# A list schedule whose assumed interval of a TensorE product is replaced by the measured one

## The chip, the cores and the metric

The kernel runs on one core of one Trainium2 chip. The metric is the device time of one execution in microseconds; a set of runs is told by its median. Five engines matter: PE (TensorE, the products and the 128x128 transposes), ACT (ScalarE), DVE (VectorE), POOL (GpSimd) and SP, which here issues nearly all DMAs. Each works through its own queue in the order in which the program was written, and waits at an instruction whose inputs are not there.

## The reference

Two layers of a decoder trunk, 1024 positions, width 1024, float32:

```python
for layer in range(DEPTH):                              # DEPTH = 2
    h = rms_norm(x, ln_mix_pre[layer])
    m = even_mixer(...) if layer % 2 == 0 else odd_mixer(...)
    x = x + rms_norm(m, ln_mix_post[layer])
    h = rms_norm(x, ln_ffn_pre[layer])
    x = x + rms_norm(swiglu(h, ffn_w_gate[layer], ffn_w_up[layer], ffn_w_down[layer]), ln_ffn_post[layer])
```

The even mixer is causal pooling beside a gated unit, the odd mixer is sparse attention (eight heads) beside chunked retention (four heads). Both begin with an input projection and end with an output projection. The hidden width of swiglu is 2816.

## The kernel before

Every product is done three times on split operands (high times high, high times low, low times high), with 512 columns wherever possible. Positions are cut into eight row blocks of 128. A projection of a row block (`proj`, line 298 for the products) is four steps of six products. The swiglu products (lines 758 and 949) use a seven-product block scheme: `hidden` works on 22 slices of the hidden width, `seven` and `down` on the way back.

Between mixer and hidden stage stands what is called a tail here (`tail`, with `halves`): for each row block the second half of the output projection is evicted (line 1102, ACT), squared for its norm (350, ACT), multiplied by the gain (420, POOL), the inverse root is taken (357, POOL), the residual is added (423, DVE) and stored (426, SP), squared and rooted again, scaled in place (441, ACT) once the store has read it, then turned by transposes (540, PE) and split (546 ACT, 547 DVE). Row blocks 4 to 7 are also subtracted from blocks 0 to 3 (555, DVE and POOL). There are two such tails, one in each layer, and a simpler one between the layers (transposes of line 372).

The order of all of this isn't written by hand. Each step is a task with an engine, an assumed duration, a priority, dependencies and buffers (`Plan.add`). `Plan.run` plays a clock forward: whenever an engine is free it takes the ready task of best priority, lets it occupy the engine for its assumed duration, and makes its result visible a fixed latency later (0.2 us for PE). The order in which the tasks were taken is the order in which they are emitted, on all engines. A task of PE that has just become ready by another engine stands back for 0.4 us (`SLACK`). So an assumed duration decides which rows stand before which, and nothing else.

The assumed durations are functions of the number of columns: `t_pe` for products, `t_turn` 0.11 us for a transpose, and

```python
def t_act(n, ptr=0, sb=0): return 0.055 + n / 1200 + 0.093 * ptr + 0.04 * sb
def t_dve(n): return 0.068 + n / 960
def t_pool(n): return 0.15 + n / 475
```

`t_pe(512, 6)` is the duration of one step of `proj`, `t_pe(512, 12)` that of one product block of `hidden`, and `core` uses `t_pe` for its score and value products. The products of retention have durations written as numbers.

Of the kernel before, what the change touches and what calls it, by code (L numbers as in the profile page):

```python
# [157 lines left out]


def t_pe(n, k=1):  # L160
    return k * max(0.086 + n / 9000, n / 2400)


def t_turn(k):
# [19 lines left out]
class Trunk:  # L184
# [115 lines left out]
    def proj(s, x, i, ws, n, deps, last, ks=((0, 1), (2, 3), (4, 5), (6, 7)), whole=True):  # L300

        q, t = s.next(), None
        for j, kk in enumerate(ks):
            wt, wh, w = ws[kk[0] // 2]

            def fn(j=j, kk=kk, w=w):
                if j == 0:
                    x["pp"] = s.bank()
                for k in kk:
                    s.mm3(x["pp"][:, :n], [s.H[z][:, i, k, :] for z in range(2)], [z[:, sl(k % 2, n)] for z in w],  # L310
                          k == ks[0][0], k == ks[-1][-1])

            first = [w_[0] for w_ in ws] if j == 0 and whole else [wt]
            t = s.add("PE", t_pe(n, 6), fn, (8, q), [t, *first] + [d for k in kk for d in deps(k)], [wh] if last else [])
            if j == 0:
                x["hp"], ho = s.hold("b", t), s.hold("og", t)
        ho.n += 1
        t.rel.append(ho)
        return t

    def projT(s, x, h, w, out, deps, last, first=True, tag="b"):

        q, t = s.next(), None
        wt, wh, w = w
        for j in range(4):
            def fn(j=j):
                if j == 0 and first:
                    x["pp"] = s.bank(tag)
                for k in (2 * j, 2 * j + 1):
                    s.mm3(out(x["pp"]), [z[:, sl(k, P)] for z in w], [s.H[z][:, 4 * h:4 * h + 4, k, :] for z in range(2)],  # L330
                          k == 0, k == KD - 1)

            t = s.add("PE", t_pe(512, 6), fn, (8, q), [t, wt] + [d for k in (2 * j, 2 * j + 1) for d in deps(k)],
                      [wh] if last else [], after=x["first"] if j == 0 and not first else None)
            if j == 0 and first:
                x["first"], x["hp"] = t, s.hold(tag, t)
            if j == 0:
                ho = s.hold("og", t)
        ho.n += 1
        t.rel.append(ho)  # L340
        return t
# [391 lines left out]
    def hidden(s, l, B):  # L733
# [5 lines left out]
        for f in range(NF):  # L739
# [10 lines left out]
            def product(wn, c, vn, o, start, deps, rel=(), first=False, x=x, w=w, tag=tag):  # L750

                def fn():
                    if first:
                        x[o] = s.bank(tag[o])
                    out = x[o]
                    for k in range(4):
                        for j, (p, v) in enumerate(((0, 0), (0, 1), (1, 0))):
                            nc.tensor.matmul(out, w[wn][p][:, c + k * P:c + (k + 1) * P], V[vn](v, k),  # L758
                                             start=start and not (k or j), stop=k == 3 and j == 2,
                                             skip_group_check=not start)  # L760

                return s.add("PE", t_pe(512, 12), fn, (8, s.next()), [*deps, *tasks[vn]], rel)
# [1630 lines left out]
```

## Time and profile before

| | us |
|---|---|
| median of 3 runs | 2293.55 (2293.12 to 2297.48) |
| profiled execution, its own time | 2297.33 |
| span of the profiled execution, first to last instruction | 2295.6 |
| PE busy in it | 2236.2 |
| DVE, ACT, POOL busy | 1500.9, 1049.7, 938.7 |

The profiled execution is 3.78 us over the median, and 1.73 us of its time lie outside the span. The program has 11008 matmul records on PE. In time order the span holds: the even mixer (to about 230 us), the tail of layer 0 (to 288), its hidden stage (to 690), the way back (to 907), the tail between the layers (to 950), the input projections of the odd mixer (to 1079), retention (to 1237), retention and attention together and attention alone (to 1548), the output projection and the tail of layer 1 (to 1663), the hidden stage and the way back (to 2296).

A row of a timeline gives the start and the length of a run of like instructions, and in brackets how long the engine had been idle before it and who released it. A matmul's length includes its run-out, so that lengths overlap; intervals are read from start to start.

### The profile page before, as it was taken

The page shows a single profiled execution, that of the slowest core. Times are in us where ns is not written, and L with a number is a line of the kernel's source. Part 1 is how long each engine was busy: PE and PEld are TensorE (multiplying, and loading weights), DVE is VectorE, ACT ScalarE, POOL GpSimd, SP SyncE. Part 2 cuts the span into 40 slices and gives each one's busy share as a digit, 9 for nine tenths or more (in the row PEclk, how much of TensorE's full clock was granted, in tenths as well). Part 3 has the DMA queues.
Part 4 walks back from the last instruction along what each step waited for, and adds up shares of the span by engine and source line. Part 5 has one row for each costly group of instructions (what it writes and reads, how often), then busy time and mean ns, then how long its engine had stood idle before and what let it go on. Part 6 is the DMA issues. An engine that isn't in the chain of part 4 may idle for free.

```text
span 2295.6 us, 30648 instructions
## 1 busy us (share of the span) xinstructions
PE 2236.2 (97%) x11008; PEld 1871.6 (82%) x11008; DVE 1500.9 (65%) x2351; ACT 1049.7 (46%) x2107; POOL 938.7 (41%) x820
## 2 busy tenths in 40 slices
PE   9999899999999999999999999999899999999998
PEld 7888778888888787788888889988778888888887
DVE  6572765656546878554665789971676565646887
ACT  4252723333334434654445778872633333335442
POOL 4431655555532422301333545541665464612323
PEclk9999999999999999999999999999999999999999
DMA  4153532333334535421341000015533232334535
GB/s 165 60 203 101 202 129 101 107 104 103 106 112 142 182 124 179 142 92 49 122 149 45 13 22 11 29 36 179 171 129 115 92 115 92 115 114 139 178 118 180
DMA packets 109017, 262.07 MB, mean 114 GB/s; under 512 B 12593, under 2 KB 20929, under 8 KB 108866
## 3 DMA queue, kind: packets, MB, share of 16 engines
q1 hardware_dynamic: 108834, 260.11, 33.6%
q8 instruction: 87, 1.43, 0.3%
q14 instruction: 64, 0.52, 0.1%
q0 software_dynamic: 32, 0.01, 0.0%
HBM read 183.80 MB, written 76.28 MB: 113 GB/s over the span
## 4 chain that ended last, share of the span: by engine, by line
PE 80%; DVE 7%; ACT 6%; issue 3%; DMA 2%; POOL 2%; SPq 0%; DVEq 0%; POOLq 0%; ACTq 0%
PE b L298 21%; PE b L758 19%; PE e L758 15%; PE b L949 7%; PE e L949 7%; PE d L2098 2%; PE b L2212 2%; PE d L298 2%; PE b L2166 2%; DVE acc L423 1%; ACT W L2125 1%; DVE H L902 1%; ACT H L2182 1%; ACT junk L350 1%; PE b L1693 1%
## 5 line engine op out<-in xcount | busy, mean ns | idle before, releaser
L298 PE MATMUL b<-W,H 128*128 128x512 f32 (+1 forms) x2508 | 595.2, 390 | 5.0 <-DVE H L547 3.5
L298 PEld LDWEIGHTS b<-W,H 128*128 128x128 f32 x2508 | 450.8, 190 | 91.6 <-DVE H L547 4.3
L758 PE MATMUL b<-H,W 128*128 128x512 f32 x1440 | 341.7, 391 | 5.9 <-ACT acc L777 5.9
L758 PEld LDWEIGHTS b<-H,W 128*128 128x128 f32 x1440 | 271.2, 188 | 63.4 <-ACT acc L777 6.8
L949 PE MATMUL b<-H,H 128*128 128x512 f32 x608 | 187.3, 389 | 0.2 <-DVE H L902 0.2
L758 PE MATMUL e<-H,W 128*128 128x512 f32 x672 | 163.0, 391 | 2.0 <-DVE H L547 1.4
L626 POOL TENSOR_TENSOR raw<-x 128x512 f32<-128x512 f32 x40 | 84.1, 2102 | 195.6 <-DVE W L614 153.6
L611 ACT ACTIVATE W<-raw 128x1024 fp32r<-128x1024 f32 x80 | 85.0, 1062 | 161.8 <-PE b L758 77.9
L758 PE MATMUL e<-T,W 128*128 128x512 f32 x608 | 157.6, 389 | 0.0
L2135 POOL TENSOR_SCALAR W<-W,rc,gates 128x640 f32<-128x640 f32 (+7 forms) x128 | 101.8, 800 | 120.4 <-DVE rc L2131 90.7
L758 PEld LDWEIGHTS e<-H,W 128*128 128x128 f32 x672 | 125.5, 188 | 28.9 <-DVE H L547 2.1
L900 ACT ACTIVATE H<-x 128x1024 fp32r<-128x1024 f32 x88 | 73.2, 873 | 161.9 <-PE e L949 79.7
L949 PE MATMUL e<-H,H 128*128 128x512 f32 x456 | 142.1, 393 | 3.5 <-DVE H L902 3.5
L597 DVE TENSOR_TENSOR x<-x,g 128x1024 f32<-128x1024 f32 x80 | 140.6, 1759 | 6.8 <-DMA x<-in_w_gu 6.8
L825 POOL TENSOR_TENSOR acc<-acc,acc 128x512 f32<-128x512 f32 x57 | 123.6, 2169 | 37.4 <-DVE acc L803 36.2
L949 PEld LDWEIGHTS b<-H,H 128*128 128x128 f32 x608 | 114.0, 188 | 24.2 <-DVE H L902 0.6
L758 PEld LDWEIGHTS e<-T,W 128*128 128x128 f32 x608 | 114.1, 188 | 23.7
L758 PE MATMUL b<-T,W 128*128 128x512 f32 x536 | 130.7, 390 | 0.2
L902 DVE TENSOR_TENSOR H<-x,H 128x1024 fp32r<-128x1024 f32 x88 | 109.6, 1261 | 32.3 <-ACT H L900 32.3
L614 DVE TENSOR_TENSOR W<-raw,W 128x1024 fp32r<-128x1024 f32 x80 | 119.2, 1490 | 17.6 <-ACT W L611 17.3
L781 DVE TENSOR_TENSOR acc<-acc,b 128x512 f32<-128x512 f32 x44 | 30.2, 686 | 152.4 <-PE b L758 109.1
L883 POOL TENSOR_TENSOR W<-W,W 128x1024 f32<-128x1024 f32 (+1 forms) x24 | 56.7, 2390 | 169.6 <-DMA W<-in_w_down 144.7
(294 smaller groups left out, 4556.9 us busy)
## 6 DMA issues: line engine op xcount, KB each, us to landing
x<-in_w_gu SPq DMA_DIRECT2D x84, 512.0 KB, 3.7
hs<-acc SPq DMA_DIRECT2D x57, 512.0 KB, 2.8
x<-hs SPq DMA_DIRECT2D x49, 512.0 KB, 3.7
W<-pw SPq DMA_DIRECT2D x28, 512.0 KB, 4.1
xd<-acc SPq DMA_DIRECT2D x24, 512.0 KB, 3.7
x<-xd SPq DMA_DIRECT2D x24, 512.0 KB, 5.6
W<-in_w_down SPq DMA_DIRECT2D x19, 512.0 KB, 6.0
x<-hs SPq DMA_DIRECT2D x35, 256.0 KB, 3.6
```

Of the source, the lines that this page charges most:

```text
L298: s.nc.tensor.matmul(out, w[p], x[q], start=first and j == 0, stop=last and j == 2)
L597: nc.vector.tensor_tensor(v, v, s.g[:, l, :, None].to_broadcast([P, KD, P]), op=OP.mult)
L611: nc.scalar.activation(w[n][0], x[src][:, cols], AF.Copy)
L614: nc.vector.tensor_sub(w[n][1], x[src][:, cols], f32(w[n][0]))
L626: nc.gpsimd.tensor_tensor(x[n][:, sl(o, 512)], y[0], y[1], op=op)
L758: nc.tensor.matmul(out, w[wn][p][:, c + k * P:c + (k + 1) * P], V[vn](v, k), start=start and not (k or j), stop=k == 3 and j == 2, skip_gr ...
L825: nc.gpsimd.tensor_tensor(ss[o[0]][:, sl(o[1], 512)], *y, op=op)
L883: e.tensor_tensor(X[n, c][:, w], X[x1, c][:, w], X[x2, c][:, w], op=OP.subtract)
L900: order = t = s.add("ACT", t_act(512 * m, sb=1), lambda: nc.scalar.activation(z[0], src()[:, :512 * m], AF.Copy), (9, q), [*deps, *fr], af ...
L902: return s.add("DVE", t_dve(512 * m), lambda: nc.vector.tensor_sub(z[1], src()[:, :512 * m], f32(z[0])), (9, q), [t], rel), q_, z
L949: nc.tensor.matmul(banks[o, p], y[u][:, 512 * k + p * P:512 * k + (p + 1) * P], w[v][:, sl(k, 512)], start=fresh and n == 1, stop=n == 3 * ...
L2135: nc.gpsimd.tensor_scalar(dst, dst, d["rc"][:, x, j:j + 1], gate, op0=OP.mult, op1=OP.mult)
```

## The change

One line. The assumed interval of a product was the larger of 0.086 + n/9000 and n/2400 us, that is 0.2133 us for 512 columns, 0.1144 for 256 and 0.1002 for 128. It becomes the larger of 0.109 and 0.0134 + n/2400, that is 0.2267, 0.1201 and 0.109.

```diff
 def t_pe(n, k=1):
-    return k * max(0.086 + n / 9000, n / 2400)
+    return k * max(0.109, 0.0134 + n / 2400)
```

No instruction is added, taken away or changed. The order changes on all five engines. On PE it is the same in the hidden stages and on the way back; it differs in the even mixer, in the three tails, in retention and attention, and at the end of attention. Three places follow, first as before, then as changed. In names, the digits behind the last underscore are a buffer's number, given in the order of emission, so the same buffer can have another number.

PE, tail of layer 0. L298 rows are steps of the output projection (b_1962 before and b_2037 in the change are row block 7, the last; b_1917 is block 6), L540 rows are transposes of finished row blocks (acc_1588 is block 4, acc_1567 is block 3), L758 rows are the first block of the hidden stage. Before:

```order
L298 MATMUL b_1917<-W_1648,H_65 128x512
L540 MATMUL b_2022<-ident,acc_1588 128x128 x4
L298 MATMUL b_1962<-W_1419,H_64 128x512
...
L298 MATMUL b_1962<-W_1636,H_64 128x512
...
L540 MATMUL b_2055<-ident,acc_1445 128x128 x4
L298 MATMUL b_1962<-W_1648,H_64 128x512
...
L540 MATMUL b_2078<-ident,acc_1567 128x128 x4
L540 MATMUL b_2089<-ident,acc_1567 128x128 x4
L758 MATMUL e_2103<-H_64,W_1664 128x512
```

In the change:

```order
L540 MATMUL b_2013<-ident,acc_1588 128x128 x4
L540 MATMUL b_2022<-ident,acc_1567 128x128 x4
L540 MATMUL b_2030<-ident,acc_1567 128x128 x4
L298 MATMUL b_2037<-W_1398,H_64 128x512
...
L540 MATMUL b_2050<-ident,acc_1445 128x128 x4
L298 MATMUL b_2037<-W_1419,H_64 128x512
...
L758 MATMUL e_2070<-H_64,W_1664 128x512
...
L540 MATMUL b_2098<-ident,acc_1621 128x128 x4
L298 MATMUL b_2037<-W_1636,H_64 128x512
...
L540 MATMUL b_2117<-ident,acc_1497 128x128 x4
L298 MATMUL b_2037<-W_1648,H_64 128x512
```

The two transposes of block 3 stood behind the last step of the projection; now they stand ahead of all four steps of row block 7. The first hidden block (12 products) and a transpose set of block 5 (acc_1621) stand ahead of its third step, a set of block 1 (acc_1497) ahead of its last. The tail of layer 1 changes in the same way.

POOL, the same tail. L420 is the gain of a row block (acc_1675 is block 7, the last), L357 an inverse root, L555 a subtraction for blocks 5 and 6. Before:

```order
L420 TENSOR_TENSOR acc_1646<-acc_1646,x_275_1728 128x1024
L357 TENSOR_TENSOR rs_2075<-ms_2041,mhalf 128x1
L357 TENSOR_TENSOR rs_2087<-ms_2060,mhalf 128x1
L420 TENSOR_TENSOR acc_1675<-acc_1675,x_275_1728 128x1024
L555 TENSOR_TENSOR acc_1621<-acc_1621 128x512
```

In the change:

```order
L420 TENSOR_TENSOR acc_1646<-acc_1646,x_275_1728 128x1024
L357 TENSOR_TENSOR rs_2068<-ms_2055,mhalf 128x1
L357 TENSOR_TENSOR rs_2087<-ms_2035,mhalf 128x1
L555 TENSOR_TENSOR acc_1621<-acc_1621 128x512
L357 TENSOR_TENSOR rs_2115<-ms_2094,mhalf 128x1
L555 TENSOR_TENSOR acc_1497<-acc_1497,acc_1621 128x512
L555 TENSOR_TENSOR acc_1646<-acc_1646 128x512
L420 TENSOR_TENSOR acc_1675<-acc_1675,x_275_1728 128x1024
```

The gain of the last row block now stands behind three subtractions of earlier blocks that it stood ahead of.

PE, end of attention. L2166 and L2168 are the last transposes of probabilities, L2212 the value products (vs of the selected branch, x of the window branch, the last of all), L298 the output projection. Before:

```order
L2166 MATMUL b_14550<-ident,W_14460 128x128
L2168 MATMUL b_14550<-ident,cp_14416 128x128
L2212 MATMUL b_14553<-H_64,vs_7152 128x256
...
L298 MATMUL b_14539<-W_13924,H_64 128x512
...
L2212 MATMUL b_14553<-H_64,x_1062_7663 128x256
```

In the change:

```order
L298 MATMUL b_14496<-W_14002,H_64 128x512
...
L2166 MATMUL b_14579<-ident,W_14483 128x128
L2168 MATMUL b_14579<-ident,cp_14451 128x128
L2212 MATMUL b_14525<-H_64,x_1062_7663 128x256
L2212 MATMUL b_14525<-H_65,x_1062_7663 128x256
```

Ten value products and a step of the projection stood between the last transposes and the last value products; now nothing does.

## Rows read from the trace of the kernel before

**Rows 1.** The page, parts 1 and 2: engines' busy time; PE in 40 slices.

```profile
PE 2236.2 (97%) x11008; PEld 1871.6 (82%) x11008; DVE 1500.9 (65%) x2351; ACT 1049.7 (46%) x2107; POOL 938.7 (41%) x820
...
PE   9999899999999999999999999999899999999998
```

**Rows 2.** Busy time in stretches; columns as the first row names them.

```profile
core 0: us, PE busy (x) PEld busy (x) DVE busy (x) ACT busy (x) POOL busy (x), PEclk, DMA share, GB/s
233.90:288.00 54.10, 47.97 (x257) 38.53 (x256) 40.63 (x60) 40.40 (x72) 34.25 (x26) 1.00 0.56 195
...
907.20:949.70 42.50, 36.75 (x186) 28.64 (x185) 36.90 (x63) 33.41 (x56) 26.72 (x21) 1.00 0.62 215
...
1603.90:1662.70 58.80, 51.41 (x265) 40.73 (x264) 39.66 (x60) 41.81 (x73) 34.76 (x27) 0.97 0.55 186
1617.60:1620.90 3.30, 3.30 (x10) 2.56 (x9) 0.39 (x3) 2.21 (x5) 1.57 (x2) 0.50 0.92 325
...
1090.40:1237.00 146.60, 146.50 (x754) 121.49 (x753) 91.36 (x276) 59.76 (x162) 48.99 (x74) 1.00 0.34 115
1237.00:1541.50 304.50, 289.15 (x2086) 264.59 (x2084) 260.62 (x674) 250.29 (x772) 150.22 (x246) 0.99 0.07 22
```

**Rows 3.** Waits of PE over the span: us in total, times, longest.

```profile
PE b L758 <- ACT acc L777: 5.9, 2, 3.0
PE b L540 <- DVE H L547: 3.9, 4, 1.5
```

**Rows 4.** The chain that ended last, in time: start, length, what.

```profile
333.92 5.44 PE b L758 x24
```

**Rows 5.** The page, part 5: groups with busy us, mean ns of one.

```profile
L626 POOL TENSOR_TENSOR raw<-x 128x512 f32<-128x512 f32 x40 | 84.1, 2102 | 195.6 <-DVE W L614 153.6
...
L781 DVE TENSOR_TENSOR acc<-acc,b 128x512 f32<-128x512 f32 x44 | 30.2, 686 | 152.4 <-PE b L758 109.1
```

**Rows 6.** Timeline of PE in the tail of layer 0.

```profile
256.63 0.66 PE L540 MATMUL b<-ident,acc 128*128 128x128 f32 x4 [1.50 <-DVE H L547]
...
260.23 1.64 PE L298 MATMUL b<-W,H 128*128 128x512 f32 x6
261.71 1.03 PE L540 MATMUL b<-ident,acc 128*128 128x128 f32 x8
...
288.03 3.34 PE L758 MATMUL e<-T,W 128*128 128x512 f32 x14
```

**Rows 7.** Timeline of ACT in the tail of layer 0.

```profile
258.86 1.14 ACT L441 ACTIVATE acc<-acc,rs 128x1024 f32<-128x1024 f32 x1
...
261.91 0.60 ACT L1102 ACTIVATE acc<-b 128x512 f32<-128x512 f32 x1 [0.32 <-PE b L298]
...
263.36 1.07 ACT L350 ACTIVATE junk<-acc 128x1024 uint8<-128x1024 f32 x1
...
278.36 1.18 ACT L441 ACTIVATE acc<-acc,rs 128x1024 f32<-128x1024 f32 x1
```

**Rows 8.** Timeline of POOL in the tail of layer 0.

```profile
264.59 2.42 POOL L420 TENSOR_TENSOR acc<-acc,x 128x1024 f32<-128x1024 f32 x1 [1.78 <-ACT junk L350]
...
273.08 1.31 POOL L555 TENSOR_TENSOR acc<-acc 128x512 f32<-128x512 f32 x1 [1.77 <-DVE acc L555]
274.40 0.55 POOL L357 TENSOR_TENSOR rs<-ms,mhalf 128x1 f32<-128x1 f32 x1
```

**Rows 9.** Timeline of DVE in the tail of layer 0.

```profile
270.09 2.31 DVE L423 SCALAR_TENSOR_TENSOR acc<-acc,rs,x 128x1024 f32<-128x1024 f32 x1 [0.44 <-POOL rs L357]
```

**Rows 10.** The page, part 6: DMA issues, KB each, us to landing.

```profile
xd<-acc SPq DMA_DIRECT2D x24, 512.0 KB, 3.7
```

**Rows 11.** Timeline of PE at the end of attention.

```profile
1541.43 0.27 PE L2168 MATMUL b<-ident,cp 128*128 128x128 f32 x1
...
1544.13 1.36 PE L2212 MATMUL b<-H,x 128*128 128x256 f32 x10
```

**Rows 12.** Timeline of DVE at the end of attention.

```profile
1542.57 0.93 DVE L2186 TENSOR_TENSOR H<-b,H 128x128 fp32r<-128x128 f32 x3 [1.05 <-ACT H L2182]
```

## The prediction

> **What bounds the kernel now.** I read the busy times and slices first [rows 1]: PE is busy 2236.2 of 2295.6 us, and every slice shows an 8 or a 9. A busy PE also counts the run-out of matmuls, so I then looked at what one product takes where nothing is waited for: 24 products in 5.44 us [rows 4], 226.7 ns each. That is the new table's figure for 512 columns (226.7) and not the old one's (213.3). So the change makes the plan's PE truer, and since only the order of emission depends on it, the time changes only where PE waits today or will wait tomorrow.
>
> The windows show where it waits [rows 2]: 54.10 - 47.97 = 6.1 us idle in the tail of layer 0, 42.50 - 36.75 = 5.8 between the layers, 58.80 - 51.41 = 7.4 in the tail of layer 1, 304.50 - 289.15 = 15.4 in attention, and 146.60 - 146.50 = 0.1 in retention. The two waits of PE over the span that belong to a tail are short [rows 3]: 3.0 us at most for the first block after it, 1.5 at most for a transpose. In the hidden stages and on the way back PE's order stays as it was, and in the even mixer PE is full (the first slices are 9s, the fifth holds the tail); those I cost at nothing.
>
> The other engines are off the path in sum (DVE 1500.9, ACT 1049.7, POOL 938.7 us, [rows 1]), but their assumed durations are too short: the plan gives a DVE pass of 512 columns 0.068 + 512/960 = 0.601 us and the trace 0.686; it gives POOL 0.15 + 512/475 = 1.228 us for 512 columns and the trace shows 2.102 for the one at line 626 [rows 5]. Before, PE's figure was too short as well (213.3 for 226.7, 6%), and part of the error cancelled. Now only the others are too fast. The plan believes that evicted, normed and split data arrive earlier, counted in products, than they do, and puts their consumers on PE earlier. That is the reason why I look for losses and not for gains.
>
> **The tail of layer 0.** Before, the last step of the output projection starts at 260.23 and takes 1.64, so it ends at 261.87; then come the two transposes of block 3 [rows 6], whose input is scaled from 258.86 to 260.00 [rows 7]. In the change these stand ahead of all four steps of row block 7. PE stops there until 260.00 and everything behind comes after it. From there to the end of the projection stand 36 products (24 of the projection, 12 of the first hidden block) and about five sets of four transposes. Eight transposes take 1.03 us and four 0.66 [rows 6], so a set in a row of others adds 0.37. 36 x 0.2267 = 8.16, plus 5 x 0.37 = 1.9, on 260.00 makes 270.1. The last step ends 8.2 us later than before.
>
> PE does useful work in most of that delay (it runs the hidden block it would have run later), so what counts is when the last row block comes back. Its chain before: eviction 261.91, 0.60; square 263.36, 1.07 [rows 7]; gain 264.59, 2.42 [rows 8]; residual 270.09 to 272.40 [rows 9]; store, 3.7 to landing [rows 10]; scale 278.36 to 279.54 [rows 7]; 17.7 us from the last product to the scaled block. This chain had waits in it: between the gain's end at 267.01 and the addition at 270.09 lie 3.1 us, and between the addition's end and the scaling 6.0, where the store takes 3.7 and the second square and root run beside it. Without queues it is 0.60 + 1.07 + 2.42 + a root of 0.55 [rows 8] + 2.31 + 3.7 + 1.18 = 11.8, and with about 0.2 at each of seven handoffs (0.16 from the square's end at 264.43 to the gain) 13.2. From 270.1 that is 283.3, some 4 us later than 279.54. The gain now stands behind three subtractions on POOL; the one before it in the profile ran 273.08 to 274.39 [rows 8], so by the time of the last gain (about 272) they may hold it for 1 to 2 us; I count this within the 0.2 us steps.
>
> What needs this block is the rest of the hidden stage's first products: before, the 14 products of 288.03 start 8.5 us after the scaling, with transposes, splits and cover between. The change takes 12 products of cover (2.7 us) to the front, so I let the whole 4 through: **+4**. Bounds: if the transposes' input comes in time and POOL is free, 0; if the 17.7 us stay as they are, 270.1 + 17.7 = 287.8, +8.3.
>
> **The tail of layer 1.** The order moves in the same way; its idle time (7.4 us) is alike: **+4**, with the same bounds.
>
> **Half clock.** At 1617.60 to 1620.90 ten products fill 3.30 us at a granted clock of 0.50, that is 1.2 GHz [rows 2]; at 226.7 ns they would be 14.6, so such a stretch costs about 1.0 us. PE's waits grow in both tails, so one more of them is likely: **+1**, from 0 (none) to +4 (two in each tail).
>
> On the interval itself the Trainium skill has a figure. Its page "TensorE: Matmul & The Clock Gate", section "Wait — 56ns, not 53.3ns?", gives 215.7 ns from start to start for 512 columns at the full clock, which is nearer to the old table than to the new one. The trace has 226.7 over 24 products [rows 4], and the measurement decides. By the page the 36 products above would end 36 x 11 = 0.4 us earlier; the sum would be 0.8 less.
>
> **Between the layers.** The first block's transposes now stand ahead of three product steps, where the plan expects their input sooner. PE waits there, and the steps it would have run fill waits that follow today. 5.8 us are idle now; I take **+0.5**, from -2 (a third of that idle time filled) to +2.
>
> **Retention.** PE has no idle time there (0.1 of 146.6), so it can't gain. Transposes and score products come earlier in the row by about one step of six products (1.36 us), where the data of DVE (91.36 us of 146.6 busy) is seldom that early. Most of it stays covered: **+1**, from 0 to +4 (three times the loss of a step).
>
> **Attention.** 15.4 us are idle, spread over some 300; 289.15 of PE against 260.62 of DVE and 250.29 of ACT, in a long loop. Here products are of 256 columns and the table changes 5% (0.1144 to 0.1201), transposes keep 0.11. The order shuffles in both directions. **0**, from -6 to +6 (40% of the idle time either way).
>
> **End of attention.** The last transposes start at 1541.43 [rows 11]; the last split by DVE ends at 1542.57 + 0.93 = 1543.50 [rows 12]. Before, ten value products and a projection step lay between and covered these 2.1 us; now the ten last value products (1.36 us for ten, [rows 11]) follow at once. About eight of them don't need the last split, about 1.0 us: 2.1 - 1.0 = **+1**, from 0 to +2.
>
> **SP.** A few reads of weights move behind stores in SP's row. Weights have buffers ahead of their use, and I cost it at 0; without that cover a read issued late by one store's 3.7 us [rows 10] would cost PE that, once or twice. This stays in the range's upper end.
>
> **Sum.** 4 + 4 + 1 + 0.5 + 1 + 0 + 1 = +11.5. On the profile's own time 2297.33 that is 2308.8; that execution is 3.78 over the median 2293.55, so the forecast for a median is 2305. The likeliest case alone runs from about 2299 to 2309.
>
> **Rivals.**
> 1. *The tails' chain keeps its length.* The last row block's 17.7 us aren't queues but latency, POOL's subtractions take the place of the waits that vanish: +8.3 in each tail, 16.6, with 1 to 4 of half clock and the other terms' 2.5 this is +20 to +23, about 2315. For it: POOL is at 34.25 of 54.10 us in the tail [rows 2], and subtractions stand ahead of the gain. Against it: 3.1 us before the addition are plainly a queue that a later block doesn't meet.
> 2. *Nothing comes of it.* When PE waits, the engines behind it work off their queues, and the next wait is shorter by as much; in the tails the hidden block that is brought forward is work that PE would have done later anyhow. Then only the end of attention and half a step here and there remain, 0 to +4, about 2295. For it: PE is 97% busy and its work is the same; the tails lose 6 to 7 us now and hold a fixed amount of cover. Against it: the cover is moved in front of the step that starts the last chain.
> 3. *Faster.* The true interval makes the long loop of attention fit: the plan's PE there is 5% slower, so fewer steps of DVE and ACT are placed as if they were late, and half of the 15.4 us idle is filled, -7.7; the tails' delay stays covered by the hidden products. With +1 at the end of attention, 2293.55 - 6.7 = 2287. It decides if PE's idle time in attention falls under about 8 us. For it: 15.4 us is the largest idle time of any stage. Against it: DVE and ACT are assumed too fast there, and a slower PE makes that worse.
>
> **How the numbers follow.** Forecast 0.48, rival 1 0.14, rival 2 0.23, rival 3 0.15. 0.2% is 4.6 us, about what a measurement of this kernel can tell from no change: faster is under 2289, slower over 2298.1. The forecast and rival 1 lie on the slower side, with a little of rival 2 (0.02): 0.64. Of rival 2 remains 0.21 and of rival 3 0.01 within 0.2%: 0.22. Faster 0.14. The range takes in most of rival 1 (to 2316) and rival 2 down to 2290, and leaves out rival 3.
>
> **What would show it.** Right: in both tails the last projection step ends 8 to 9 us later, PE waits in front of block 3's transposes and again before the first products that need row block 7, and the hidden stage of layer 0 starts its even run about 4 us later; PE's idle time rises in the tails, not in the hidden stages; at the end of attention a wait of about 1 us for a split by DVE. Wrong: the last step ends later but the hidden stage starts as before (rival 2); the wait for row block 7 grows by 8 (rival 1); attention's span falls by more than 6 us (rival 3). If the time moves in a hidden stage or on a way back, where PE's order is unchanged, my reading is wrong altogether.

## The result, and the profile after

| | before | with the change |
|---|---|---|
| median, us | 2294.57 (4 runs, 2293.12 to 2297.48) | 2309.91 (4 runs, 2307.09 to 2312.32) |
| profiled execution, own time (span) | 2297.33 (2295.6) | 2307.09 (2305.4) |

The ratio is 1.0066, with a 95% interval of 1.0051 to 1.0081: 15 us slower. The two profiled executions lie only 9.8 us apart, since that of before is its slowest of four and that of the change its fastest. Single executions of one order differ by 4 to 9 us (23 runs of before beside the last experiments lie between 2290.61 and 2299.78); stages are therefore priced by medians, and the traces are read for places.

Of the page, PE's busy time (before in [rows 1]), and of part 5 two groups that answer to [rows 5]:

```profile
PE 2232.3 (97%) x11008; PEld 1869.5 (81%) x11008; DVE 1489.0 (65%) x2351; ACT 1051.7 (46%) x2107; POOL 916.4 (40%) x820
...
L626 POOL TENSOR_TENSOR raw<-x 128x512 f32<-128x512 f32 x40 | 71.1, 1778 | 222.6 <-DVE W L614 183.7
...
L781 DVE TENSOR_TENSOR acc<-acc,b 128x512 f32<-128x512 f32 x44 | 30.2, 687 | 151.1 <-PE b L758 107.8
```

PE does the same work in 9.8 us more. Its waits over the span (us in total, times, longest), against [rows 3]:

```profile
PE b L758 <- ACT acc L777: 7.4, 2, 3.7
PE b L2166 <- DVE H L2186: 6.8, 9, 2.3
PE b L298 <- DVE H L1377: 6.7, 1, 6.7
...
PE b L540 <- DVE H L547: 4.4, 2, 2.4
```

The third is new as a large one, and it stands in the even mixer. The same wait in a timeline of PE, before and after (start, length, what, in brackets the idle time before it and who ended it):

```profile
140.18 4.29 PE L298 MATMUL b<-H,W 128*128 128x512 f32 x18
145.16 0.97 PE L298 MATMUL b<-v,W 128*128 128x512 f32 x3 [0.69 <-DVE H L1377]
```

```profile
140.51 4.29 PE L298 MATMUL b<-H,W 128*128 128x512 f32 x18
151.46 2.90 PE L298 MATMUL b<-v,W 128*128 128x512 f32 x6 [6.66 <-DVE H L1377]
```

0.69 us of waiting have become 6.66, and the six products behind the wait take 2.70 us to the next start instead of 1.36. The stages by windows (columns as in [rows 2]; the same stretches, moved by what the trace is late there):

```profile
138.00:152.00 14.00, 7.34 (x31) 5.73 (x30) 14.00 (x14) 9.00 (x16) 9.35 (x6) 0.90 0.46 187
240.80:294.90 54.10, 47.18 (x256) 37.93 (x254) 35.75 (x58) 40.90 (x71) 33.19 (x26) 1.00 0.54 195
914.60:957.10 42.50, 36.80 (x186) 28.80 (x186) 36.57 (x66) 34.37 (x57) 26.84 (x21) 1.00 0.62 217
1612.40:1671.20 58.80, 52.27 (x279) 42.17 (x278) 36.50 (x60) 43.57 (x76) 33.15 (x26) 1.00 0.52 185
```

In the tails PE is idle about as long as before (6.9 us for 6.1, 6.5 for 7.4), between the layers too (5.7 for 5.8). The first row is the new hole, with the granted clock at 0.90 in its mean. The stretch at 0.50 that [rows 2] shows in the tail of layer 1 is not there (1.00 in the last row).

To follow the loss along the span I compared, in the two traces, when PE starts the work that stands behind the same sum of product intervals (0.2267 us for 512 columns, 0.120 for 256, 0.109 for 128). Late by, in us, positive where the change is later:

| up to | late by |
|---|---|
| the even mixer before the wait | -1.0 |
| its output projection | +6.9 |
| first hidden products (about 290 us) | +7.2 |
| even run of the hidden stage (from 350) | +9.4 |
| end of the way back | +7.4 |
| projections of the odd mixer | +5.7 |
| attention, first part (1320) | +2.8 |
| attention, 80 us before its end | +4.5 |
| output projection of layer 1 | +8.5 |
| hidden stage of layer 1 | +8.8 |
| end | +9.8 |

So in this pair the even mixer costs 8 us, the tail of layer 0 with the first hidden slices 2.5, the end of attention 4, the tail of layer 1 next to nothing, and the odd mixer gives 4 to 5 back before its end. The 2.0 us by which the change catches up on the way back of layer 0 are mostly clock: before has PE at a granted clock of 0.50 from 771.00 to 774.40, and the trace of the change has no such stretch there.

### The profile page after: what moved, and what is told of

Its sections match the earlier page's. It is cut to its first block, busy times and chain, and to the rows that moved or that the text cites. A ratio compares the mean times of both kernels' runs of the same rounds, so it can differ in the third digit from the quotient of the medians.

```text
span 2305.4 us, 30667 instructions
## 1 busy us (share of the span) xinstructions
PE 2232.3 (97%) x11008; PEld 1869.5 (81%) x11008; DVE 1489.0 (65%) x2351; ACT 1051.7 (46%) x2107; POOL 916.4 (40%) x820
## 5 line engine op out<-in xcount | busy, mean ns | idle before, releaser
L298 PE MATMUL b<-W,H 128*128 128x512 f32 (+1 forms) x2508 | 594.9, 389 | 1.9 <-ACT H L377 1.2
L298 PEld LDWEIGHTS b<-W,H 128*128 128x128 f32 x2508 | 449.3, 189 | 86.6 <-ACT H L377 1.6
L758 PE MATMUL b<-H,W 128*128 128x512 f32 x1440 | 343.2, 392 | 7.4 <-ACT acc L777 7.4
L758 PEld LDWEIGHTS b<-H,W 128*128 128x128 f32 x1440 | 272.4, 189 | 65.1 <-ACT acc L777 8.3
L758 PE MATMUL e<-H,W 128*128 128x512 f32 x672 | 162.5, 391 | 2.4 <-DVE acc L781 2.4
L626 POOL TENSOR_TENSOR raw<-x 128x512 f32<-128x512 f32 x40 | 71.1, 1778 | 222.6 <-DVE W L614 183.7
L758 PE MATMUL e<-T,W 128*128 128x512 f32 x608 | 157.9, 389 | 0.0
L597 DVE TENSOR_TENSOR x<-x,g 128x1024 f32<-128x1024 f32 x80 | 143.2, 1794 | 13.5 <-DMA x<-in_w_gu 13.3
L758 PEld LDWEIGHTS e<-H,W 128*128 128x128 f32 x672 | 125.5, 188 | 29.2 <-DVE acc L781 3.2
L758 PEld LDWEIGHTS e<-T,W 128*128 128x128 f32 x608 | 114.0, 188 | 23.6
L758 PE MATMUL b<-T,W 128*128 128x512 f32 x536 | 130.2, 389 | 0.0
L614 DVE TENSOR_TENSOR W<-raw,W 128x1024 fp32r<-128x1024 f32 x80 | 117.6, 1470 | 14.8 <-ACT W L611 14.8
L902 DVE TENSOR_TENSOR H<-x,H 128x1024 fp32r<-128x1024 f32 x88 | 102.9, 1184 | 34.8 <-ACT H L900 34.8
```

Source lines behind the costliest of these rows:

```text
L298: s.nc.tensor.matmul(out, w[p], x[q], start=first and j == 0, stop=last and j == 2)
L597: nc.vector.tensor_tensor(v, v, s.g[:, l, :, None].to_broadcast([P, KD, P]), op=OP.mult)
L614: nc.vector.tensor_sub(w[n][1], x[src][:, cols], f32(w[n][0]))
L626: nc.gpsimd.tensor_tensor(x[n][:, sl(o, 512)], y[0], y[1], op=op)
L902: return s.add("DVE", t_dve(512 * m), lambda: nc.vector.tensor_sub(z[1], src()[:, :512 * m], f32(z[0])), (9, q), [t], rel), q_, z
```

## The experiments

**One stage at a time.** Both intervals are kept for each product task, and the plan uses the new one only for a range of PE's 1581 tasks; outside it the order of every engine is that of before, inside that of the change.

```diff
 def t_pe(n, k=1):
-    return k * max(0.109, 0.0134 + n / 2400)
+    return Both(k * max(0.086 + n / 9000, n / 2400), k * max(0.109, 0.0134 + n / 2400))
...
-                    push(best, "end", now + best.dur)
+                    n += eng == "PE"
+                    dur = float(best.dur) if n < 155 else float(getattr(best.dur, "old", best.dur))
+                    push(best, "end", now + dur)
```

The condition is `n < 155` in only_even, `155 <= n < 420` in only_tail0, `420 <= n < 1255` in only_odd and `n >= 1255` in only_tail1.

only_even: 

> The new interval is used for the first 155 tasks of PE (through the even mixer, into its output projection), the old one behind; the order is that of the change up to there and that of before behind. Theory of the trace (a wait of 6.7 us before a product of the pooled branch): +6 to +8 us. Theory of the prediction (PE is full there, nothing happens): 0, within 2.

only_tail0: 

> The new interval is used for PE's tasks 155 to 419 only (tail and hidden stage of layer 0). Theory of the prediction: +4 to +5 us. Theory of the trace (the last projection step comes some 5 us later, but hidden products cover it, and about 2.5 us come from waits and half clock in the first hidden slices): +1 to +3.5.

only_odd: 

> The new interval is used for PE's tasks 420 to 1254 only (tail between the layers, projections of the odd mixer, retention, attention). Theory of the prediction: +2.5 us (0.5 + 1 + 0 + 1). Theory of the trace: losses at the end of attention of about 4 and gains before it of about 5, so -3 to +1.

only_tail1: 

> The new interval is used for PE's tasks from 1255 on (tail of layer 1 and what follows). Theory of the prediction: +4 to +5 us. Theory of the trace: +0 to +3. If the four runs add up to the whole difference (+15 us of the medians) the stages act each for itself; if they stay at about +10 (the difference of the two profiled executions), the rest lies in the spread of executions.

Measured against 2295.27 us of before (27 runs beside them):

| | median, us | difference | ratio, 95% interval |
|---|---|---|---|
| only_even | 2301.76 | +6.5 | 1.0027, 1.0015 to 1.0038 |
| only_tail0 | 2298.36 | +3.1 | 1.0017, 1.0008 to 1.0026 |
| only_odd | 2296.11 | +0.8 | 1.0005, 0.9996 to 1.0014 |
| only_tail1 | 2298.24 | +3.0 | 1.0015, 1.0006 to 1.0024 |

The differences add up to 13.4, the ratios to 1.0064; the whole change has 1.0066. Each difference is known to about 2 us; as far as that tells, the stages act each for itself. All four lie where the reading of the trace had put them, and the even mixer, priced at nothing in the prediction, is the largest.

**What the wait in the even mixer is made of.** VectorE from the last common point to the result that PE waits for (line 1377), in the change, and POOL beside it:

```profile
139.72 4.08 DVE L692 TENSOR_TENSOR acc<-x,acc 128x512 fp32r<-128x512 f32 x3
143.72 1.77 DVE L1340 TENSOR_TENSOR m<-m,gl 128x512 f32<-128x512 f32 x1
145.42 3.43 DVE L1360 TENSOR_TENSOR H<-m,H 128x512 fp32r<-128x512 f32 x2
148.77 0.68 DVE L1367 TENSOR_TENSOR v<-acc,v 128x512 fp32r<-128x512 f32 x1
...
150.58 0.74 DVE L1377 SCALAR_TENSOR_TENSOR H<-b,psc,H 128x512 fp32r<-128x512 f32 x1
```

```profile
141.58 1.68 POOL L704 TENSOR_TENSOR x<-x 128x512 f32<-128x512 f32 x1 [0.64 <-DVE acc L692]
143.33 3.29 POOL L704 TENSOR_TENSOR x<-x,x 128x512 f32<-128x512 f32 x2
146.70 1.60 POOL L704 TENSOR_TENSOR x<-x 128x512 f32<-128x512 f32 x1
```

Lines 685, 692 and 704 prepare the first two hidden slices ahead of time, work of the lowest priority. In the change the first of the three splits (the second slice's) stands ahead of VectorE's chain, and once it is done POOL's four sums start, at 141.58. Until they end at 148.30 the passes of 512 columns on VectorE take 1.7 us from start to start; from 148.77 on they take 0.60. POOL's passes start 1.7 us apart as well (141.58, 143.33, 146.70 with one between), where one alone is 1.3 us long, as if the two engines took turns. Before, that split ran at 151.81 and the sums behind it:

```profile
141.35 0.68 DVE L1360 TENSOR_TENSOR H<-m,H 128x512 fp32r<-128x512 f32 x1
141.95 0.68 DVE L1367 TENSOR_TENSOR v<-acc,v 128x512 fp32r<-128x512 f32 x1
...
144.36 0.74 DVE L1377 SCALAR_TENSOR_TENSOR H<-b,psc,H 128x512 fp32r<-128x512 f32 x1
```

To part the queue from the overlap, even_sums_late keeps the order of only_even on VectorE up to the wait, and puts a small copy on POOL in front of the sums that reads VectorE's late result:

```diff
+                if (h, g) == (0, 2):
+                    def gate():
+                        nc.gpsimd.tensor_copy(s.pad, f32(Hk(1, 2, 0))[:, 0, :8])
+                    t = s.add("POOL", 0.2, gate, (0, q), [Y[h, g]])
+                    t.users.append(s.first_sum)
+                    s.first_sum.wait += 1
```

> Like only_even (new interval for the first 155 PE tasks, order of the change there), but POOL's four sums of the second prepared slice (line 704 of the change) are held back: POOL first copies 8 columns of a result that VectorE's chain delivers last (line 1377), and the sums stand behind that copy. VectorE's order up to the wait is unchanged. Theory 'overlap' (VectorE takes about 1.75 us instead of 0.68 for 512 columns while POOL runs its sums, and this makes the wait of 6.7 us): the wait shrinks to 0.5 to 2 us and the time comes down to before +0 to +3 us. Rival 'queue' (the three splits of line 692 that now stand ahead on VectorE make the wait by themselves): the wait stays above 4 us and the time at +5 to +7.

Its timelines of VectorE, POOL and PE (line numbers 14 higher):

```profile
139.51 2.98 DVE L706 TENSOR_TENSOR acc<-x,acc 128x512 fp32r<-128x512 f32 x3
142.42 0.68 DVE L1354 TENSOR_TENSOR m<-m,gl 128x512 f32<-128x512 f32 x1
143.02 1.28 DVE L1374 TENSOR_TENSOR H<-m,H 128x512 fp32r<-128x512 f32 x2
...
146.03 0.74 DVE L1391 SCALAR_TENSOR_TENSOR H<-b,psc,H 128x512 fp32r<-128x512 f32 x1
```

```profile
146.84 0.58 POOL L1406 COPY pad<-H 128x8 f32<-128x8 f32 x1 [6.10 <-DVE H L1391]
147.38 1.27 POOL L718 TENSOR_TENSOR x<-x 128x512 f32<-128x512 f32 x1
```

```profile
146.92 0.94 PE L312 MATMUL b<-v,W 128*128 128x512 f32 x3 [2.33 <-DVE H L1391]
```

And its busy times behind the wait (columns as in [rows 2]):

```profile
148.50:151.90 3.40, 3.40 (x10) 2.62 (x9) 3.40 (x3) 2.33 (x5) 3.24 (x3) 0.50 0.05 19
```

The same instructions on VectorE take 7.3 us (139.51 to 146.77) instead of 11.6 (139.72 to 151.32), and PE's wait is 2.33 us, not 6.66. So 4.3 us of the wait are the overlap with POOL, and about 1.6 (2.33 less the 0.69 of before) the queue. The median is 2297.24 against 2293.57, +3.7, ratio 1.0018 (1.0010 to 1.0027): under only_even's +6.5, though the intervals overlap. Both figures miss what 'overlap' expected (a wait of 0.5 to 2 us, 0 to +3), and both are clear of 'queue'. What the +3.7 holds beyond the wait is the clock: PE runs at a granted 0.50 from 148.50 to 151.90, and in this trace it is 3.6 us later behind the even mixer than ahead of it, 1.6 of them wait. Further on, the order of 30 products and some rows of the other engines differs from only_even's. The overlap is shown in the trace; its price in the time only roughly.

**The end of attention.** odd_to_1130 is only_odd with the condition `420 <= n < 1130`.

> The new interval for PE's tasks 420 to 1129 only: tail between the layers, odd mixer and attention up to about 80 us before its end, old interval at the end of attention and behind it. Theory 'end of attention' (only_odd won about 3 us up to there and lost 4 to 5 in the last 70 us): -4 to -1 us against before. Theory of the prediction (end of attention costs 1): +0.5 to +1.5. Rival 'chance' (every cut of the order moves the time by some us at random): outside -4 to +1.5.

2290.58 us against 2293.57: ratio 0.9986 (0.9977 to 0.9995), 3 us faster than before. Up to 80 us before its end the new order of the odd mixer is a gain; the last part costs some 4 us (+0.8 for only_odd, -3.0 here). There, between 1470 and 1565 us, PE's waits add up to 5.8 us in the change and in only_odd, to 2.1 before and to 1.5 in odd_to_1130. The longest in the change, and what follows it:

```profile
1512.29 0.63 PE L2166 MATMUL b<-ident,W 128*128 128x128 f32 x4 [2.35 <-DVE H L2186]
...
1516.30 1.63 PE L298 MATMUL b<-W,H 128*128 128x512 f32 x6
...
1521.34 1.55 PE L298 MATMUL b<-W,H 128*128 128x512 f32 x6
```

Steps of the output projection, the only filler, stand at 1516 and 1521 already; before, the first of them starts at 1527.62. I held that for the cause. odd_filler_late makes them wait in the plan for a late transpose:

```diff
+        for a, b in ((4568, 4673), (4568, 4678)):
+            s.tasks[a].users.append(s.tasks[b])
+            s.tasks[b].wait += 1
```

> Like only_odd, but in the plan the first steps of two row blocks of the output projection wait for a late transpose of attention, so that eight steps (1.36 us each) are left for its last 20 us, as before. Theory 'cover spent early' (in the change four of these steps stand up to 12 us earlier, and PE waits 1 to 2 us three or four times in the last 40 us): 2 to 4 us less than only_odd, -3 to -1 against before. Rival 'no cover to spare' (the steps only move the wait to the stretch that loses them): within 1 us of only_odd.

2295.96 against 2294.83, ratio 1.0001 (0.9993 to 1.0010), and by the median difference (+1.1) no better than only_odd, as the rival has it. In its trace the first of these steps stands at 1528.89 and the waits near the end are gone, but others stand ahead of them: 5.1 us in all, and the wait of 2.3 us is still there (2.36). The theory falls, although the interval still reaches 1.6 us below before. VectorE shows what stands ahead of the split that PE waits for, in the change:

```profile
1509.01 1.56 DVE L282 TENSOR_TENSOR W<-raw,W 128x1024 fp32r<-128x1024 f32 x1
1510.49 0.81 DVE L2107 TENSOR_REDUCE mx<-d 128x1 f32<-128x640 f32 x1
1511.22 1.83 DVE L2186 TENSOR_TENSOR H<-b,H 128x128 fp32r<-128x128 f32 x5
```

A weight split and a maximum stand before it. That they make the loss was not tried.

**The tail of layer 0.** tail0_turns_late is only_tail0 with the plan's constraint that block 3's transposes and the first hidden block wait for the last projection step (pairs 568 to 667, 670 and 783, in the same loop as above).

> Like only_tail0, but in the plan block 3's two sets of transposes and the first hidden block wait for the last step of the output projection, so that row block 7's steps stand ahead of them again, as before. Theory of the prediction (what stands ahead of row block 7 makes the last block late): from only_tail0's +3 to +4 us down to 0 to +1.5. Rival 'other engines' (the cost comes from VectorE's changed order in the tail and in the first hidden slices, which stays): +2.5 to +4.

2298.75 against 2294.83: +3.9, ratio 1.0019 (1.0010 to 1.0029). That is where the rival has it and clear of the 0 to +1.5: with row block 7's steps put ahead again the cost is not smaller. That VectorE's order makes it, as the rival says, this run doesn't show.

**Why a truer interval makes a worse plan.** Three theories were tried on the table alone.

```diff
 def t_act(n, ptr=0, sb=0):
-    return 0.055 + n / 1200 + 0.093 * ptr + 0.04 * sb
+    return 1.06 * (0.055 + n / 1200 + 0.093 * ptr + 0.04 * sb)
 def t_dve(n):
-    return 0.068 + n / 960
+    return 1.06 * (0.068 + n / 960)
 def t_pool(n):
-    return 0.15 + n / 475
+    return 1.06 * (0.15 + n / 475)
```

This is all_plus_6; in all_measured the factors are 1.05, 1.27 and 1.3.

all_plus_6: 

> The new interval for PE over the whole program and the assumed durations of ACT, DVE and POOL times 1.06, so that the proportion of the engines is that of before. Theory 'proportion' (the change makes the other engines look too fast beside PE): between -3 and +4 us against before. Rival 'any other table is worse than the one the kernel had, by chance': +5 to +15, as the change.

all_measured: 

> The new interval for PE and the assumed durations of the other engines near their means in the trace: ACT times 1.05, DVE times 1.27, POOL times 1.3. Theory 'proportion': no slower than before, perhaps 2 to 6 us faster, no wait over 3 us in the even mixer. Rival 'chance': +5 to +15. A third case: means do not help, since a slow VectorE is slow only beside POOL: within 4 us of before.

2302.20 and 2322.91 us against 2293.57: ratios 1.0040 (1.0026 to 1.0054) and 1.0126 (1.0113 to 1.0140). The proportion of the engines is not the reason. The plan whose durations were moved towards the trace's means is the worst of all, 29 us slower, which none of its three expectations covers. It loses most in attention, where PE is busy for 230.00 of 250 us; in the same part of before it is busy for 240.25:

```profile
1300.00:1550.00 250.00, 230.00 (x1671) 209.16 (x1671) 211.46 (x519) 199.45 (x582) 120.84 (x181) 1.00 0.07 20
```

```profile
1290.00:1540.00 250.00, 240.25 (x1768) 222.44 (x1767) 219.88 (x547) 210.26 (x618) 126.27 (x193) 0.99 0.06 20
```

Then the interval the other way, `k * max(0.095, n / 2480)` in interval_low and `k * max(0.09, n / 2600)` in interval_lower:

interval_low: 

> The change's line with an interval 9% shorter than measured (0.2065 us for 512 columns, 3% under that of before), nothing else. Theory 'direction' (a longer interval of PE brings the consumers of other engines' results forward and uncovers them, a shorter one puts them back): -5 to +2 us against before. Rival 'chance' (any other table gives another order, and that of before is one of the better ones): +3 to +15.

interval_lower: 

> The change's line with an interval of 0.1969 us for 512 columns, 8% under that of before, nothing else. In the even mixer this order again puts a split of the second prepared slice ahead of VectorE's chain, as the change does and interval_low does not. Theory 'direction' (the shorter the interval of PE, the more cover): -15 to -5 us against before. Theory 'single places' (each table decides at a few places, as in the even mixer, whether work on POOL meets VectorE's chain or cover is spent early, and the sum has no direction): the wait in the even mixer comes back with 4 us or more, and the time lies above interval_low's -10, between -6 and +10.

interval_low: 2284.84 us against 2294.83, ratio 0.9948 (0.9935 to 0.9961), 10 us faster than before and the best of all; neither expectation covers that. interval_lower: 2297.53 against 2293.90, ratio 1.0016 (1.0007 to 1.0025). There is no direction. At 0.2267, 0.2133, 0.2065 and 0.1969 us for 512 columns the time stands at +15, 0, -10 and +4. In the even mixer, PE before the same products in interval_low and interval_lower:

```profile
144.90 1.57 PE L298 MATMUL b<-v,W 128*128 128x512 f32 x6
```

```profile
148.76 1.65 PE L298 MATMUL b<-v,W 128*128 128x512 f32 x3 [5.36 <-DVE H L1377]
```

The long wait is there exactly where the order puts the second slice's split ahead of VectorE's chain, at 0.2267 and at 0.1969, and not in between. That speaks for single places, as the last expectation had it. Compared as in the table above, interval_lower leaves the even mixer (228 us) 11.5 us later than it came to this place (143 us), interval_low 0.3: most of the 13 us between them. The gain of interval_low lies elsewhere, though: in its trace 8.8 us come between 1237 and 1320 us of before, where retention and attention run together. A part of them is a stretch at a granted clock of 0.50 that before has there (1252.30 to 1255.70); what in the order makes the rest was not tried.

## Why the prediction was right, and where it was not

The forecast was 2305 with +11.5; measured are 2309.9 and +15.3. The sign and the range held. The terms held less well, and that the sum came so near is luck in good part: the stages that it priced at 11.5 gave 3.1 + 3.0 + 0.8 = 6.9, and the even mixer, which it had at nothing, gave 6.5. Of the signs that were to show it right, the wait for VectorE's last splits at the end of attention is there (0.82 us). The last projection step of layer 0 comes 5.3 us later and not 8 to 9, PE doesn't wait for block 3, its idle time in the tails is about as before, and the even run of the hidden stage starts 2.5 us later, not 4.

**The step that failed** is the sentence that in the even mixer "PE is full" and that its changed order costs nothing. It costs +6.5 alone (only_even), 4 tenths of the whole. That PE is full says that nothing can be won there; it does not say that VectorE's chain, for which PE waits 0.69 us even before the change, cannot be made later still by work of the lowest priority put ahead of it. That split moves in VectorE's order, and I read only PE's.

**Tails.** +4 each was forecast, +3.1 and +3.0 measured: near in size, but not for the reason given. The last step of layer 0's projection starts at 272.42 and ends at 274.05; less the 6.9 us of the even mixer that is 267.15, 5.3 later than before, not 8.2:

```profile
261.18 1.75 PE L540 MATMUL b<-ident,acc 128*128 128x128 f32 x12
...
272.42 1.63 PE L298 MATMUL b<-W,H 128*128 128x512 f32 x6
...
318.38 3.02 PE L758 MATMUL e<-H,W 128*128 128x512 f32 x12 [1.27 <-DVE acc L781]
335.99 4.62 PE L758 MATMUL b<-H,W 128*128 128x512 f32 x12 [3.70 <-ACT acc L777]
```

PE doesn't wait for block 3 at all. I had taken 260.00 from [rows 7] as the time at which its input is ready, but that time belongs to the old order: in the change the block is scaled from 259.42 to 260.57, less 6.9 that is 253.7. The chain of the last block, which I worked out as 13.2 us without queues against 17.7, came out right in its sum:

```profile
259.42 1.15 ACT L441 ACTIVATE acc<-acc,rs 128x1024 f32<-128x1024 f32 x1
...
286.39 1.15 ACT L441 ACTIVATE acc<-acc,rs 128x1024 f32<-128x1024 f32 x1 [0.50 <-DMA xd<-acc]
```

```profile
276.43 2.40 POOL L420 TENSOR_TENSOR acc<-acc,x 128x1024 f32<-128x1024 f32 x1
```

```profile
282.35 1.27 DVE L423 SCALAR_TENSOR_TENSOR acc<-acc,rs,x 128x1024 f32<-128x1024 f32 x1
```

287.54 - 274.05 = 13.5. Its parts differ: the addition starts 3.5 us behind the gain's end (278.83), where a root of 0.55 and handoffs were counted, but it takes 1.27 and not 2.31, and from its end to the scaling it is 2.8 us, where the store alone was put at 3.7. So the block is scaled only 1.1 us later than before (280.6 for 279.54), and tail0_turns_late shows that its place is not what costs. In only_tail0's trace 3.3 of the 5.3 us lost by 350 us come after 290 us, in the first hidden slices, where I had said that a loss would make my reading "wrong altogether". For the tail that sign came true: PE's order is unchanged there, VectorE's is not. In the change two scalings follow each other,

```profile
313.19 4.55 DVE L597 TENSOR_TENSOR x<-x,g 128x1024 f32<-128x1024 f32 x2
317.66 0.67 DVE L781 TENSOR_TENSOR acc<-acc,e 128x512 f32<-128x512 f32 x1
```

each at 2.3 us beside POOL, and the eviction that PE waits for at 318.38 stands behind both; before it stood between them (scaling at 305.95, eviction at 308.19, scaling at 308.78). This reading fits the rows; no run took that one pair apart. It explains a wait of some 1.2 us. Another part of only_tail0's loss is half clock, at 280.80 to 284.20 and here, where before has only 327.30 to 330.70:

```profile
328.60:335.40 6.80, 5.69 (x13) 4.47 (x14) 3.84 (x3) 2.05 (x4) 6.16 (x4) 0.50 0.27 107
```

**Odd mixer.** 0.5 + 1 + 0 + 1 = +2.5 was forecast, +0.8 measured (0.9996 to 1.0014), as the sum of -3 and +4. The end of attention, for which I looked at the last ten value products alone, costs 4 and not 1; the loss lies spread over its last 70 us. The term for attention itself, 0 from -6 to +6, held by its bounds.

**Half clock.** One stretch more was forecast, for the tails, at 1.0 us. The price was read too low: the ten products of [rows 2] include those that lie over an edge of the window. The twelve that begin there take 4.44 us to the next start (1621.58) and not 2.72, so such a stretch costs 1.7:

```profile
1617.14 4.60 PE L298 MATMUL b<-W,H 128*128 128x512 f32 x12 [1.88 <-DVE H L547]
```

In the change this one is gone, and a longer one stands in the even mixer: behind the 6.66 us wait six products take 2.70 us, and of the 8 us lost there about 2 are clock. In sum the two profiled executions are alike, with a mean granted clock of 0.996 each. The medians are not. The four executions of the change have 0.996, 0.995, 0.993 and 0.992, at 2307.09, 2308.77, 2311.05 and 2312.32 us, which is 1.3 us more for each 0.001 less; their mean is 0.994, and that of the 86 executions of before beside the experiments 0.9963. By that rate half clock makes about 3 of the 15.3 us, an estimate: more than the +1, within its bounds. These 3 us are no stage of their own; they are part of what the stages cost.

**The reason given for looking for losses** falls. I held 0.686 us of [rows 5] against the plan's 0.601 for a VectorE pass. The first is a length with its run-out; from start to start it is 0.60 (141.35 to 141.95 above), as planned. The 2.102 of POOL at line 626 isn't one duration either: its passes of 512 columns take from 1.3 us to 2.3. How long a pass takes depends on what the other engine does beside it, which no mean can tell a plan, and all_measured shows what using means does. Rival 3, a gain in attention, was half there: -3 in odd_to_1130, though not from PE's interval as such, since other tables win or lose it too.

## What to carry to other kernels

The durations of a list scheduler are knobs of its order: a truer number gives another order, not a better one, and is to be measured like any other change. When such an order changes, look on every engine for work of low priority that has moved ahead of a chain with little slack, and ask what it starts on an engine that shares a path with the chain; a stage in which the bound engine is full can still lose. A wait of that engine can cost more than its length, where its clock is at half behind it. And a ready time read from the old trace holds only for what does not move.

## What the runs showed of the hardware

VectorE passes with both inputs in SBUF can slow down beside POOL's: 512 columns from 0.60 us start to start (0.68 long) to 1.7 (1.75 long) at line 1360, 1024 columns from 1.23 to 2.3 long at line 597. With one input in PSUM they don't: line 781 keeps 0.67 at 317.66 while POOL's line 626 runs from 316.61 to 318.87:

```profile
316.61 2.26 POOL L626 TENSOR_TENSOR raw<-x,x 128x512 f32<-128x512 f32 x1
```

The Trainium skill says this in kind on the page "GPSIMD Engine Reference", section "Key points": POOL shares its SBUF interfaces with VectorE, and they get in each other's way where a VectorE instruction has two SBUF inputs. The rows agree and add the size, a factor of 1.9 to 2.8; the page gives none. POOL pays too: 1.27 to 1.30 us for 512 columns where VectorE leaves it alone, up to 2.26 beside it.

Not every such pass is slow. In the hidden stages of the change the passes of line 614 over 512 columns start just ahead of a pass of POOL; 34 of the 40 keep 0.69 us, and POOL's takes 1.78 in place of 1.29:

```profile
439.31 0.69 DVE L614 TENSOR_TENSOR W<-x,W 128x512 fp32r<-128x512 f32 x1
```

```profile
439.38 1.78 POOL L626 TENSOR_TENSOR raw<-x,raw 128x512 f32<-128x512 f32 x1
```
